# A hybrid decoder layer on one core: block differences on VectorE alone, earlier weight sums and loads, an earlier first w_down split, last rows scaled in two steps

## The chip, the cores and the metric

The kernel runs on one core of a Trainium2 chip. The metric is the device time in microseconds (us). TensorE is PE in the profile's rows (PEld: its weight loads), VectorE is DVE, ScalarE is ACT, GpSimd is POOL, SyncE is SP. A q behind a name (SPq, ACTq) is the engine's sequencer, which issues DMAs.

## The reference, cut to what matters

One layer works on 1024 prompt rows and 32 sample rows together, 1056 rows of 1024 columns in float32. `g_mix` here stands for the three gated branches.

```
x = x + g_mix @ w_o                                   # 1024 x 1024
h = rmsnorm(x, norm_ffn_g) @ w_up                     # 1024 x 5632
hc = dwconv3_causal(h) + conv_f_b ; a, g = split(hc)
x = x + (silu(g) * a) @ w_down                        # 2816 x 1024
y = rmsnorm(x, norm_final_g)
```

## The kernel before, in words

**Precision.** Each float32 operand is split in a high part (ScalarE rounds it: `hi`) and a low part (VectorE subtracts: `lo`), and `three` (L210 to L213) makes a product of three matmuls: high by high, high by low, low by high. For a unit of w_in, w_o or w_down the split is `split_unit`: cast L188 on ScalarE, subtraction L190 on VectorE, which waits in `lows` until `split_lows` issues it.

**W_o.** The 1056 columns are four quarters of 264. 32 steps (`wo_step`, 24 matmuls each) run in the order of the loop at L1536: quarters 0 and 2 first (s = 0, steps 0 to 15), then 1 and 3 (s = 1, steps 16 to 31). The result is added to x in S (L1297 for two quarters of one row block, L1308 for two row blocks of one quarter); ScalarE squares it (L1299, L1302, L1310) and GpSimd or VectorE sums the squares into `acc` (L1303, L1313). `todo` holds what else is issued at a point (step, third of the step): parts of the norm, the first weight loads, sums and splits.

**The norm and z's blocks.** `norm2(c)` makes the second RMSNorm of quarter c: `total` (six tiny matmuls L1217 that sum `acc`, then a short chain L1218 to L241 on VectorE), `spread` (L1229, the scale across partitions), four `scale` items (two L1257 each). w_up is multiplied by a Strassen-like scheme with seven products per pair of halves, so z's four blocks b11, b12, b21, b22 (S, four row blocks by one quarter) are subtracted from each other (`minus`, L1251, four per pair of quarters) and split (`parts`: cast L1246, subtraction L1247). s = 0 stands for quarters 0 and 2, s = 1 for 1 and 3. In norm2(2) all four `minus` are GpSimd's, in norm2(3) two of them.

**W_up.** `entries` holds (j, quarters): the first four are (0, s=0), (1, s=0), (0, s=1), (1, s=1), then j = 2 to 21 with both. Each entry has seven products in the ORDER 1, 2, 6, 5, 7, 3, 4: 12 matmuls each in entries 0 to 3, 24 after that. For each entry `raw_load` fetches four pieces of 256 KB of w_up, `sums` makes the weight sums on GpSimd (L1354 to L1356, and L1371 later), `prepare` splits each weight (L1367 on ScalarE, L1368 on VectorE) three products ahead. `evacuate` reads the result out of PSUM (L1463 on ScalarE for product 1, L1461 on VectorE for the rest); the PSUM tile `pair` has three buffers, so product i + 3 waits for the evacuation of product i. The convolution's taps (L1420, L1424), the gate (L1436, L1437, L1441) follow from a queue `late`.

**W_down.** During the last entry `at_last` loads the first units of w_down and stages the first activations from memory (`loads`) and splits them (`splits`: L1605, L1606). Then 24 units of 24 (or 12) matmuls per 352 columns run, three times. `ahead` splits two units ahead.

**The last rows.** `turn` transposes the result (L1687) and squares it (L1690), `scales` makes the factors, `out` scales by the row's factor and by norm_final_g (`gfin`): L1715 on VectorE, or L1719 on ScalarE followed by L1720 on GpSimd, and stores.

Each engine works in the order of issue; the code is written in the order in which it issues.

Of the kernel before, what the change touches and what calls it, by code (L numbers as in the profile page):

```python
# [9 lines left out]
F32 = mybir.dt.float32  # L10
# [5 lines left out]
P = 128  # L16
D = 1024
# [40 lines left out]
def layer_step(ctx: ExitStack, tc: tile.TileContext, I, O):  # L58
# [297 lines left out]
    with tc.manual_schedule():  # L356
# [848 lines left out]
        def norm2(c):  # L1205
# [56 lines left out]
            if not second:  # L1262
                return total, spread, [
                    scale(0, 0), scale(0, 1), scale(1, 0), scale(1, 1), parts(1, b11), parts(2, b21)
                ]
            dve = nc.vector if s else nc.gpsimd
            return total, spread, [
                scale(0, 0), scale(0, 1),
                minus(b11, b12, b11, dve),
                scale(1, 0), scale(1, 1),  # L1270
                parts(3, b22),
                minus(b12, b22, b12, nc.gpsimd),
                minus(b22, b22, b11, dve),
                parts(6, b22),
                parts(5, b11),
                minus(b21, b21, b22, nc.gpsimd),
                parts(7, b12),
                parts(4, b21),
            ]
# [42 lines left out]
        def raw_load(e):  # L1322
            if e > last or e in raw:
                return
            j = entries[e][0]
            raw[e] = []
            for half in range(2):
                if half and e >= 4:
                    t = v3(S[:, 6 + e % 2, :], KT, P)
                else:  # L1330
                    t = ring.tile([P, KT, P], F32, name="ws", tag="ws", bufs=3)
                t = t[:, 0:4, :], t[:, 4:8, :]
# [28 lines left out]
        def prepare(upto):  # L1361
            while prepared[0] < min(upto, len(steps)):
                e, n = steps[prepared[0]]
                a = raw[e][n]
                t = ring.tile([P, KT, P], F32R, name="wh", tag=("wh", "wl")[prepared[0] % 2], bufs=3)
                hi, lo = t[:, 0:4, :], t[:, 4:8, :]
                nc.scalar.copy(out=hi, in_=a)  # L1367
                nc.vector.tensor_tensor(out=lo, in0=a, in1=f32(hi), op=ALU.subtract)  # L1368
                wform[e, n] = hi, lo
                if n == 1:  # L1370
                    nc.gpsimd.tensor_tensor(out=a, in0=raw[e][2], in1=raw[e][6], op=ALU.subtract)  # L1371
                    if e >= 4:
                        raw_load(e + 1)
                if n == 3 and e < 4:
                    raw_load(e + 1)
                if n == 7 and e >= 4 or n == 4 and e < 4:
                    sums(e + 1)
                if n == 4:
                    raw.pop(e)
                    if e == 0:  # L1380
                        fs.put(wsum.pop(e))
                prepared[0] += 1
# [67 lines left out]
        def evacuate(e, n, ps):  # L1450
            j, ss = entries[e]
            a, m = ss[0], len(ss)
            u = as4(S[:, 2 + e % 2, :]) if e >= 4 else block(S, e % 2 if e < 2 else 0, 2)
            ps = ps[:, a : a + m, :QC]
            s1, u2 = u[:, a : a + m, :], u[:, 2 + a : 2 + a + m, :]

            def cols(half, c):
                at = 2 + (c + a) * QC
                return hb_get(j, half)[:, at : at + m * QC].rearrange("p (s t) -> p s t", t=QC)

            add = lambda out, x: nc.vector.tensor_tensor(out=out, in0=ps, in1=x, op=ALU.add)  # L1461
            if n == 1:
                nc.scalar.copy(out=s1, in_=ps)  # L1463
            elif n == 6:
                add(u2, s1)
            elif n == 2:
                add(cols(0, 0), s1)
            elif n == 5:
                add(s1, u2)
            elif n == 7:  # L1470
                add(cols(1, 2), s1)
                add(u2, u2)
            elif n == 3:
                add(cols(0, 2), s1)
            else:
                add(cols(1, 0), u2)
# [19 lines left out]

        norms = {c: norm2(c) for c in range(4)}

        def plan_norm(at, c, first=0):

            total, spread, items = norms[c]
            slots = {(at, 2): [total], (at + 1, 2): [spread]}
            for i, x in enumerate(items):
                slots[at + 2 + i // 3, i % 3] = [x]
            return slots

        todo = {}
        for at, c in ((12, 0), (16, 2), (28, 1)):
            for key, gos in plan_norm(at, c).items():
                todo.setdefault(key, []).extend(gos)  # L1510
        todo.setdefault((24, 0), []).append(lambda: sums(0))
        todo.setdefault((22, 2), []).append(lambda: raw_load(0))
        for i in range(6):
            todo.setdefault((25 + i // 2, i % 2), []).append(lambda i=i: prepare(i + 1))

        def wo_step(at, w, ps, c):
            wh, wl = w
# [106 lines left out]
        def at_last(n):  # L1624

            if n == 1:
                for c in range(3):
                    for q, g in down_order(c):
                        k0, nk = kg[g]
                        unit_cols(w_down, q * 256, k0=k0, nk=nk, cols=256)  # L1630
            go = {
                1: [load_unit, load_unit, loads[0]],
                5: [lambda: extra_free(6), splits[0], loads[1]],
                7: [lambda: rows_free(0), load_unit, loads[2]],
                3: [splits[1], loads[3], splits[2], loads[4], split_unit],
                4: [lambda: extra_free(7), splits[3], split_lows, loads[5]],
            }
# [5 lines left out]
        ffn_first[1] = [total]  # L1643
# [22 lines left out]


        gfin = fs.get()
        nc.sync.dma_start(out=gfin[:, :D], in_=I["norm_final_g"].partition_broadcast(P))
        extra_free(4)  # L1670
        rows_free(4)

        def finish(c):
# [25 lines left out]
            def scales(a, z):  # L1699
# [3 lines left out]
                    rsqrt(ms, y, tmp, P)  # L1703
                return go

            def out(i, parts=((0, D, True),)):
                def go():
                    t0, n = PIECES[3 * c + i]
# [16 lines left out]
                    fs.put(y)  # L1725
                return go

            return turn, scales, out

        left = list(late)  # L1730
        late.clear()
        for c in range(3):
            turn, scales, out = finish(c)
            work = {}

            def at_slot(q, g, *gos):
# [5 lines left out]
            if c == 0:  # L1742
# [5 lines left out]
                at_slot(0, 4, loads[7])  # L1748
                at_slot(1, 1, splits[7])
                at_slot(1, 2, x_again)  # L1750
            else:
                x_again()
                for i in range(3):
# [14 lines left out]
            for q, g in down_order(c):  # L1768
# [34 lines left out]
        turn, scales, out = before  # L1803
# [42 lines left out]
```

## Time and profile before

| | us |
|---|---|
| median of 3 runs | 1890.14 (1888.81 to 1891.46) |
| the profiled execution | 1889.29 |
| its span in the trace | 1887.5 |
| TensorE busy in the span | 1831.9 |
| W_o, steps 28 to 31, up to W_up's first product | 1098 to 1121 |
| W_up's entries 0 to 3 | 1121 to 1187 |
| W_up's entries 4 to 23 | 1187 to 1602 |
| W_down and the last rows | 1602 to 1887.5 |

The span is counted from the first instruction; the execution's own time is 1.8 us longer. The page shows TensorE nearly full; so the reader looks for stretches in which it is not, and there at who ended its waits. "PEclk" is the clock that was granted to TensorE, 1.00 at full speed.

### The profile page before, as it was taken

The page shows a single profiled execution, that of the slowest core. Times are in us where ns is not written, and L with a number is a line of the kernel's source. Part 1 is how long each engine was busy: PE and PEld are TensorE (multiplying, and loading weights), DVE is VectorE, ACT ScalarE, POOL GpSimd, SP SyncE. Part 2 cuts the span into 40 slices and gives each one's busy share as a digit, 9 for nine tenths or more (in the row PEclk, how much of TensorE's full clock was granted, in tenths as well). Part 3 has the DMA queues.
Part 4 walks back from the last instruction along what each step waited for, and adds up shares of the span by engine and source line. Part 5 has one row for each costly group of instructions (what it writes and reads, how often), then busy time and mean ns, then how long its engine had stood idle before and what let it go on. Part 6 is the DMA issues. An engine that isn't in the chain of part 4 may idle for free. (4 is left out here: it accounts for less than half of the span.)

```text
span 1887.5 us, 31072 instructions
## 1 busy us (share of the span) xinstructions
PE 1831.9 (97%) x12576; PEld 1807.1 (96%) x12576; DVE 1159.2 (61%) x2144; ACT 640.9 (34%) x1045; POOL 384.8 (20%) x475
## 2 busy tenths in 40 slices
PE   8999999999999999999999987999999999899997
PEld 8988999999999999999999986999999999899997
DVE  5577676337633483328436477888988897655433
ACT  6654313221232123211324233334333334444332
POOL 2231100000000000000000344566556654000000
PEclk9999999999999999999999988999999999899999
DMA  8736252125221422133316221323222222776642
GB/s 260 214 106 206 73 175 86 56 68 169 68 59 45 147 93 77 44 120 107 92 35 193 71 79 58 91 71 91 76 74 86 78 79 94 236 230 228 202 156 90
DMA packets 252204, 216.08 MB, mean 114 GB/s; under 512 B 7958, under 2 KB 237150, under 8 KB 252062
## 3 DMA queue, kind: packets, MB, share of 16 engines
q1 hardware_dynamic: 241860, 200.01, 34.3%
q10 hardware_dynamic: 10201, 14.10, 2.2%
q8 instruction: 99, 1.62, 0.3%
q14 instruction: 44, 0.35, 0.1%
HBM read 184.27 MB, written 29.81 MB: 113 GB/s over the span
## 5 line engine op out<-in xcount | busy, mean ns | idle before, releaser
L211 PE MATMUL mm<-zhi,wh 128*128 128x352 f32 x1728 | 560.9, 325 | 0.3 <-ACT zhi L273 0.3
L212 PE MATMUL mm<-zlo,wh 128*128 128x352 f32 x1728 | 558.1, 323 | 1.0 <-POOL zlo L284 1.0
L213 PE MATMUL mm<-zhi,wl 128*128 128x352 f32 x1728 | 557.7, 323 | 0.2 <-DVE wl L190 0.2
L190 DVE TENSOR_TENSOR wl<-ws,wh 128x1024 fp32r<-128x1024 f32 x183 | 223.3, 1222 | 221.9 <-ACT wh L188 221.6
L211 PE MATMUL pair<-zhi,wh 128*128 128x264 f32 (+1 forms) x1096 | 326.0, 297 | 14.1 <-DVE rs L1461 8.8
L212 PEld LDWEIGHTS mm<-zlo,wh 128*128 128x128 f32 x1728 | 324.5, 188 | 2.2 <-POOL zlo L284 1.6
L211 PEld LDWEIGHTS mm<-zhi,wh 128*128 128x128 f32 x1728 | 325.0, 188 | 1.1 <-ACT zhi L273 0.6
L213 PEld LDWEIGHTS mm<-zhi,wl 128*128 128x128 f32 x1728 | 324.6, 188 | 0.5 <-DVE wl L190 0.5
L212 PE MATMUL pair<-zlo,wh 128*128 128x264 f32 (+1 forms) x1096 | 322.9, 295 | 0.0
L188 ACT CAST wh<-ws 128x1024 fp32r<-128x1024 f32 (+1 forms) x184 | 187.3, 1020 | 256.6 <-PE pair L212 97.5
L211 PEld LDWEIGHTS pair<-zhi,wh 128*128 128x128 f32 x1096 | 207.2, 189 | 17.3 <-issue 15.3
L212 PEld LDWEIGHTS pair<-zlo,wh 128*128 128x128 f32 x1096 | 207.5, 189 | 0.0
L213 PE MATMUL pair<-zhi,wh 128*128 128x264 f32 x704 | 201.3, 286 | 0.0
L213 PEld LDWEIGHTS pair<-zhi,wh 128*128 128x128 f32 x704 | 133.9, 190 | 0.0
L211 PE MATMUL pair<-fs,wh 128*128 128x264 f32 (+1 forms) x396 | 119.8, 303 | 3.1 <-ACT wh L188 2.7
L213 PE MATMUL pair<-zhi,wl 128*128 128x352 f32 (+1 forms) x392 | 121.4, 310 | 0.0
L212 PE MATMUL pair<-fs,wh 128*128 128x264 f32 (+1 forms) x396 | 118.5, 299 | 0.0
L844 DVE CUSTOM_DVE_ANT_0 qr<-fs,fs 128x256 f32<-128x256 f32 x256 | 108.4, 424 | 7.3
L211 PE MATMUL pair<-rs,wh 128*128 128x264 f32 (+1 forms) x352 | 104.7, 297 | 4.3 <-DVE rs L1461 3.2
L212 PE MATMUL pair<-rs,wh 128*128 128x264 f32 (+1 forms) x352 | 104.8, 298 | 0.0
L1130 ACT ACTIVATE sig<-mm 128x352 f32<-128x352 f32 x72 | 33.4, 465 | 187.2 <-PE mm L213 186.7
L1143 DVE TENSOR_TENSOR sig<-sig,fs 128x352 f32<-128x352 f32 x48 | 25.2, 525 | 108.0 <-ACT sig L1130 108.0
(333 smaller groups left out, 3276.1 us busy)
## 6 DMA issues: line engine op xcount, KB each, us to landing
ws<-in_w_in SPq DMA_DIRECT2D x88, 512.0 KB
ws<-in_w_down SPq DMA_DIRECT2D x60, 512.0 KB
fs<-q_d SPq DMA_DIRECT2D x32, 512.0 KB
ws<-in_w_up SPq DMA_DIRECT2D x56, 256.0 KB
S<-in_w_up SPq DMA_DIRECT2D x40, 256.0 KB
fs<-in_cache_mem_k SPq DMA_DIRECT2D x16, 512.0 KB
fs<-in_cache_mem_v SPq DMA_DIRECT2D x16, 512.0 KB
act_d<-fs SPq DMA_DIRECT2D x13, 528.0 KB
```

The costliest lines, as they stand in the source:

```text
L188: nc.scalar.copy(out=hi, in_=t)
L190: lows.append(lambda: eng.tensor_tensor(out=lo, in0=t, in1=f32(hi), op=ALU.subtract))
L211: mmul(ps, lhsT=wh, rhs=xh, start=first, stop=False)
L212: mmul(ps, lhsT=wh, rhs=xl, start=False, stop=False)
L213: mmul(ps, lhsT=wl, rhs=xh, start=False, stop=last)
L844: nc.vector.tensor_tensor_reduce(out=att["qr"], in0=q[:, i, :], in1=t[:, 2 * (bb % 2) + mt, :], scale=1.0, scalar=0.0, op0=ALU.mult, op1=A ...
L1130: nc.scalar.activation(out=t, in_=ps, func=AF.Sigmoid)
L1143: nc.vector.tensor_tensor(out=t, in0=t, in1=src[:, r], op=ALU.mult)
```

## The change

- All four `minus` of norm2(2) and norm2(3) are on VectorE.
- `todo` is written point by point: norm2(2)'s items come two per step (from step 18); `raw_load(0)` at step 20, `sums(0)` at step 21, the first six splits at steps 22 to 27, `raw_load(1)` at step 25, `sums(1)` at step 27. norm2(1)'s total moves from behind step 28 into step 29, its spread from behind step 29 into step 30; its two `parts` move behind W_up's products 0 and 1.
- The second halves of the raw weights of entries 1 and 2 lie in S instead of the ring `ws`, so `raw_load(2)` and `raw_load(3)` are issued one entry earlier than before. `sums` of entries 2, 3 and 4 are issued with product 7 (before: product 4 up to entry 3).
- In the last entry of W_up the first unit of w_down is split at product 7 and the second at product 3 (before: the first at product 3, behind two staged pieces, its low part at product 4).
- norm_final_g is loaded in the last quarter of W_down's first third instead of at its start.
- The last three row blocks: VectorE multiplies the first 768 columns by norm_final_g as soon as they are transposed (`scaled`), and the row's factor follows at the end (`out_end`), on ScalarE for the first and third block and on VectorE for the second; the last 256 columns stay in one step on VectorE. All stores are SyncE's.

The last few line numbers shift: L1367 and L1368 are L1371 and L1372 after, L1354 to L1356 are L1358 to L1360, L1371 is L1375, L1461 is L1465, L1605 and L1606 are L1616 and L1617.

```diff
-            dve = nc.vector if s else nc.gpsimd
+            dve = nc.vector
...
-                minus(b12, b22, b12, nc.gpsimd),
+                minus(b12, b22, b12, dve),
                 minus(b22, b22, b11, dve),
...
-                minus(b21, b21, b22, nc.gpsimd),
+                minus(b21, b21, b22, dve),
...
-                if half and e >= 4:
-                    t = v3(S[:, 6 + e % 2, :], KT, P)
+                if half and e in (1, 2):
+                    t = block(S, 1, 4 - 2 * e)
+                    t = t[:, :, 0:P], t[:, :, P : 2 * P]
...
-                    if e >= 4:
+                    if e >= 3:
                         raw_load(e + 1)
-                if n == 3 and e < 4:
-                    raw_load(e + 1)
-                if n == 7 and e >= 4 or n == 4 and e < 4:
+                if n == 3 and e < 2:
+                    raw_load(e + 2)
+                if n == 7 and e:
                     sums(e + 1)
...
-            u = as4(S[:, 2 + e % 2, :]) if e >= 4 else block(S, e % 2 if e < 2 else 0, 2)
+            u = as4(S[:, 2 + e % 2, :]) if e >= 4 else block(S, 0, 2)
...
+        plan_norm(0, (12, 2), (13, 2), [(14, 0), (14, 0), (14, 1), (14, 2), (15, 0), (15, 1)])
+        plan_norm(2, (16, 2), (17, 2), [(18 + i // 2, i % 2) for i in range(13)])
+        rest1 = plan_norm(1, (29, 0), (30, 0), [(30, 1), (30, 2), (31, 0), (31, 1)])
+        at_point(20, 0, lambda: raw_load(0))
+        at_point(21, 2, lambda: sums(0))
...
-                7: [lambda: rows_free(0), load_unit, loads[2]],
-                3: [splits[1], loads[3], splits[2], loads[4], split_unit],
-                4: [lambda: extra_free(7), splits[3], split_lows, loads[5]],
+                7: [lambda: rows_free(0), load_unit, loads[2], split_unit, split_lows],
+                3: [splits[1], loads[3], split_unit, split_lows, splits[2], loads[4]],
+                4: [lambda: extra_free(7), splits[3], loads[5]],
...
+            def scaled(i):
+
+                def go():
+                    n = PIECES[3 * c + i][1]
+                    b = tiles[i][:n].rearrange("p h x -> p (h x)")
+                    nc.vector.tensor_tensor(
+                        out=yo[i][:n, : 6 * P], in0=b[:, : 6 * P], in1=gfin[:n, : 6 * P], op=ALU.mult
+                    )
+                return go
...
+                at_slot(3, 4, gfin_load)
...
                     turn(g - 1, 0, 6)()
+                    scaled(g - 1)()
...
         for i in range(3):
-            out(i, ((0, 512, True), (512, D, i == 2)))()
+            out_end(i)
```

VectorE's order in W_o from step 18 on (S holds x and z, zlo and fs_… the low parts of z's blocks, wh on the left the low part of a weight):

```order
-L1257 SCALAR_TENSOR_TENSOR S<-S,vec,aux 128x264 x8
+L1257 SCALAR_TENSOR_TENSOR S<-S,vec,aux 128x264 x4
+L1251 TENSOR_TENSOR S<-S 128x4x264
+L1257 SCALAR_TENSOR_TENSOR S<-S,vec,aux 128x264 x2
 L1297 TENSOR_TENSOR S<-pair,S 128x2x264
+L1257 SCALAR_TENSOR_TENSOR S<-S,vec,aux 128x264 x2
 L1247 TENSOR_TENSOR zlo<-S,zhi 128x4x264
+L1251 TENSOR_TENSOR S<-S 128x4x264 x2
+L1297 TENSOR_TENSOR S<-pair,S 128x2x264
 L1247 TENSOR_TENSOR fs_10242<-S,fs_10241 128x1056
+L1372 TENSOR_TENSOR wh<-ws,wh 128x512
```

The differences L1251 have entered VectorE's queue between the scalings and the low parts, and the first split weight (L1372) stands ahead of W_o's later additions L1297.

GpSimd's order at the same place (fs_9653 is `acc`, ws the raw weights, fs_10374 and fs_10447 the sums of entry 0):

```order
 L1313 TENSOR_TENSOR fs_9653<-fs_9653,fs_9654 128x264 x4
-L1251 TENSOR_TENSOR S<-S 128x4x264
+L1303 TENSOR_TENSOR fs_9653<-fs_9653,fs_9654 128x2x264 x2
+L1358 TENSOR_TENSOR fs_10374<-ws 128x4x128
+L1359 TENSOR_TENSOR fs_10374<-fs_10374,ws 128x4x128
+L1360 TENSOR_TENSOR ws<-ws 128x512
+L1375 TENSOR_TENSOR ws<-ws,fs_10374 128x512
 L1303 TENSOR_TENSOR fs_9653<-fs_9653,fs_9654 128x2x264
-L1251 TENSOR_TENSOR S<-S 128x4x264 x3
-L1303 TENSOR_TENSOR fs_9653<-fs_9653,fs_9654 128x2x264 x2
-L1354 TENSOR_TENSOR fs_10447<-ws 128x4x128
-L1355 TENSOR_TENSOR fs_10447<-fs_10447,ws 128x4x128
```

Four differences have left GpSimd's queue, and the sums of entry 0 stand ahead of the third of the additions L1303.

VectorE's order at the end of W_up, before (zlo and rs_… on the left of L1606 are low parts of staged activations, wl those of w_down's units, fs_16047 and rs_16151 results of the last entry):

```order
L1461 TENSOR_TENSOR S<-pair,S 128x528
L1461 TENSOR_TENSOR rs_16151<-pair,S 128x528
L1461 TENSOR_TENSOR S<-pair,S 128x528
L1606 TENSOR_TENSOR rs_10795<-S,rs_10794 128x1056
L1606 TENSOR_TENSOR zlo<-S,zhi 128x1056
L1441 TENSOR_TENSOR rs_16016<-rs_16016,S 128x1056
L1461 TENSOR_TENSOR fs_16047<-pair,S 128x528
L1606 TENSOR_TENSOR zlo<-S,zhi 128x1056
L190 TENSOR_TENSOR wl<-ws,wh 128x1024
L1461 TENSOR_TENSOR rs_16151<-pair,S 128x528
L190 TENSOR_TENSOR wl<-ws,wh 128x1024 x2
L1420 SCALAR_TENSOR_TENSOR fs_16197<-fs_16047,vec,fs_16197 128x1024
```

And the same stretch after:

```order
L1465 TENSOR_TENSOR S<-pair,S 128x528
L190 TENSOR_TENSOR wl<-ws,wh 128x1024
L1465 TENSOR_TENSOR rs_16153<-pair,S 128x528
L1465 TENSOR_TENSOR S<-pair,S 128x528
L1617 TENSOR_TENSOR rs_10799<-S,rs_10798 128x1056
L190 TENSOR_TENSOR wl<-ws,wh 128x1024
L1617 TENSOR_TENSOR zlo<-S,zhi 128x1056
L1445 TENSOR_TENSOR rs_16014<-rs_16014,S 128x1056
L1465 TENSOR_TENSOR fs_16045<-pair,S 128x528
L1617 TENSOR_TENSOR zlo<-S,zhi 128x1056
L1465 TENSOR_TENSOR rs_16153<-pair,S 128x528
L190 TENSOR_TENSOR wl<-ws,wh 128x1024
```

The low part of the first unit has moved ahead of product 7's two evacuations, that of the second ahead of the second staged piece; the third still stands behind product 4's evacuation and just ahead of the convolution's taps.

More of the change, by code (lines that the diff above doesn't have):

```diff
@@ L1327, in raw_load @@
             for half in range(2):
-                if half and e >= 4:
-                    t = v3(S[:, 6 + e % 2, :], KT, P)
-                else:
-                    t = ring.tile([P, KT, P], F32, name="ws", tag="ws", bufs=3)
-                t = t[:, 0:4, :], t[:, 4:8, :]
+                if half and e in (1, 2):
+                    t = block(S, 1, 4 - 2 * e)
+                    t = t[:, :, 0:P], t[:, :, P : 2 * P]
+                else:
+                    if half and e >= 4:
+                        t = v3(S[:, 6 + e % 2, :], KT, P)
+                    else:
+                        t = ring.tile([P, KT, P], F32, name="ws", tag="ws", bufs=3)
+                    t = t[:, 0:4, :], t[:, 4:8, :]
                 c0 = half * FF + j * P
@@ L1497, in layer_step, with at_point, plan_norm @@
         norms = {c: norm2(c) for c in range(4)}
-        def plan_norm(at, c, first=0):
+        todo = {}
+        def at_point(step, i, go):
+            todo.setdefault((step, i), []).append(go)
+        def plan_norm(c, t, s, points):
             total, spread, items = norms[c]
[L1502 to L1514, printed above, removed]
+            at_point(*t, total)
+            at_point(*s, spread)
+            for x, point in zip(items, points):
+                at_point(*point, x)
+            return items[len(points) :]
+        plan_norm(0, (12, 2), (13, 2), [(14, 0), (14, 0), (14, 1), (14, 2), (15, 0), (15, 1)])
[3 more added lines that the diff above has]
+        at_point(21, 2, lambda: sums(0))
+        for i, point in enumerate([(22, 0), (23, 0), (24, 1), (25, 0), (26, 0), (27, 0)]):
+            at_point(*point, lambda i=i: prepare(i + 1))
+        at_point(25, 0, lambda: raw_load(1))
+        at_point(27, 1, lambda: sums(1))
         def wo_step(at, w, ps, c):
@@ L1642, in layer_step @@
         total, spread, items = norms[3]
-        ffn_first[1] = [total]
+        ffn_first[0] = rest1[:1]
+        ffn_first[1] = [total, *rest1[1:]]
         ffn_first[3] = [spread]
@@ L1668, in layer_step, with gfin_load @@
         gfin = fs.get()
-        nc.sync.dma_start(out=gfin[:, :D], in_=I["norm_final_g"].partition_broadcast(P))
+        def gfin_load():
+            nc.sync.dma_start(out=gfin[:, :D], in_=I["norm_final_g"].partition_broadcast(P))
         extra_free(4)
@@ L1704, in scales, with out_end @@
                 return go
+            def scaled(i):
[6 more added lines that the diff above has]
+                return go
+            def out_end(i):
+                t0, n = PIECES[3 * c + i]
+                b = tiles.pop(i)[:n].rearrange("p h x -> p (h x)")
+                y, ri = yo.pop(i), st["y3"][:n, i : i + 1]
+                m = min(n, NP - t0)
+                if i % 2:
+                    nc.vector.tensor_scalar(
+                        out=y[:n, : 6 * P], in0=y[:n, : 6 * P], scalar1=ri, scalar2=1.0, op0=ALU.mult, op1=ALU.mult
+                    )
+                else:
+                    nc.scalar.activation(out=y[:n, : 6 * P], in_=y[:n, : 6 * P], func=AF.Copy, scale=ri)
+                nc.vector.scalar_tensor_tensor(
+                    out=y[:n, 6 * P : D], in0=b[:, 6 * P : D], scalar=ri, in1=gfin[:n, 6 * P : D],
+                    op0=ALU.mult, op1=ALU.mult,
+                )
+                for fr in (slice(0, 6 * P), slice(6 * P, D)):
+                    nc.sync.dma_start(out=O["y_prompt"][0, t0 : t0 + m, fr], in_=y[:m, fr])
+                    if m < n:
+                        nc.sync.dma_start(out=O["y_sample"].rearrange("b t d -> (b t) d")[:, fr], in_=y[m:n, fr])
             def out(i, parts=((0, D, True),)):
@@ L1726, in out @@
                 return go
-            return turn, scales, out
+            return turn, scales, out, scaled, out_end
         left = list(late)
@@ L1732, in layer_step @@
         for c in range(3):
-            turn, scales, out = finish(c)
+            turn, scales, out, scaled, out_end = finish(c)
             work = {}
@@ L1802, in layer_step @@
             before = turn, scales, out
-        turn, scales, out = before
         for i in range(3):
```

## The prediction

> **What bounds the kernel now.** I read the page first, then busy time by stage, then TensorE's waits.
>
> ```profile
> span 1887.5 us, 31072 instructions
> PE 1831.9 (97%) x12576; PEld 1807.1 (96%) x12576; DVE 1159.2 (61%) x2144; ACT 640.9 (34%) x1045; POOL 384.8 (20%) x475
> ```
>
> TensorE is busy 1831.9 of 1887.5 us, so only 55.6 us can come from waits. Busy time by stage (columns: PE, PEld, DVE, ACT, POOL busy, granted clock, DMA share, GB/s) shows where they lie.
>
> ```profile
> 1100.00:1122.00 22.00, 15.06 (x105) 14.88 (x104) 13.28 (x24) 5.05 (x9) 6.37 (x6) 0.77 0.28 85
> 1122.00:1187.00 65.00, 47.56 (x343) 46.16 (x342) 50.98 (x82) 25.48 (x41) 32.20 (x31) 0.87 0.24 69
> 1200.00:1600.00 400.00, 400.00 (x3258) 397.94 (x3257) 346.57 (x448) 149.59 (x220) 230.75 (x283) 1.00 0.26 79
> 1600.00:1630.00 30.00, 22.30 (x128) 21.79 (x127) 25.57 (x25) 16.48 (x16) 6.88 (x13) 0.83 0.72 226
> 1630.00:1860.00 230.00, 230.00 (x1450) 229.70 (x1449) 110.28 (x129) 85.25 (x101) 0.10 (x1) 1.00 0.63 202
> ```
>
> From 1200 to 1600 and from 1630 to 1860 TensorE never stops: 0.123 us per matmul of 264 columns (400/3258), 0.159 of 352 (230/1450). The change can win only at W_o's end (6.9 idle in 22), in W_up's entries 0 to 3 (17.4 in 65), where W_down begins (7.7 in 30), and in the last rows. In the first three the clock is below 1 too. TensorE's waits name who was late:
>
> ```profile
> PE pair L211 <- DVE rs L1461: 12.0, 4, 7.4
> PE aux L1217 <- DVE fs L1313: 6.9, 1, 6.9
> PE pair L213 <- DVE wl L190: 5.0, 1, 5.0
> PE pair L211 <- ACT wh L188: 2.7, 1, 2.7
> PE aux L1229 <- DVE y L241: 1.4, 1, 1.4
> ```
>
> Each is VectorE (once ScalarE). So the question is not what TensorE does but when VectorE's queue reaches L1313, L1461 and L190. Two things hold that queue up. First, GpSimd:
>
> ```profile
> 1073.40 2.49 POOL L1251 TENSOR_TENSOR S<-S 128x1056 f32<-128x1056 f32 x1 [15.04 <-DVE S L1257]
> 1077.65 8.57 POOL L1251 TENSOR_TENSOR S<-S 128x1056 f32<-128x1056 f32 x3
> 1096.34 1.74 POOL L1354 TENSOR_TENSOR fs<-ws 128x512 f32<-128x512 f32 x1
> 1098.15 1.63 POOL L1355 TENSOR_TENSOR fs<-fs,ws 128x512 f32<-128x512 f32 x1
> 1146.73 1.26 POOL L1356 TENSOR_TENSOR ws<-ws 128x512 f32<-128x512 f32 x1
> ```
>
> ```profile
> 1084.80 2.54 DVE L1247 TENSOR_TENSOR fs<-S,fs 128x1056 fp32r<-128x1056 f32 x1 [6.00 <-ACT fs L1246]
> 1087.26 1.25 DVE L1247 TENSOR_TENSOR zlo<-S,zhi 128x1056 fp32r<-128x1056 f32 x1
> 1095.45 3.17 DVE L1368 TENSOR_TENSOR wh<-ws,wh 128x512 fp32r<-128x512 f32 x2 [1.28 <-ACT wh L1367]
> 1105.47 0.69 DVE L1308 TENSOR_TENSOR S<-pair,S 128x528 f32<-128x528 f32 x1
> 1107.01 0.90 DVE L1313 TENSOR_TENSOR fs<-fs,fs 128x264 f32<-128x264 f32 x2 [0.84 <-ACT fs L1310]
> ```
>
> L1247 takes 1.25 us with GpSimd idle and 2.54 while the last L1251 runs (to 1086.2); then the two L1368 (0.68 each elsewhere) take 3.17 between L1303, L1354 and L1355, which stretch to 1.74 and 1.63 from about 1.26. I read this as turns: operations with both inputs in SBUF on VectorE and GpSimd run one after the other, and with both queues full they alternate. Second, late weights:
>
> ```profile
> 1144.10 1.31 POOL L1354 TENSOR_TENSOR S<-ws 128x512 f32<-128x512 f32 x1 [12.08 <-DMA ws<-in_w_up]
> 1150.38 2.30 DVE L1251 TENSOR_TENSOR S<-S 128x1056 f32<-128x1056 f32 x1 [6.08 <-POOL S L1251]
> 1153.82 2.89 DVE L1247 TENSOR_TENSOR rs<-S,rs 128x1056 fp32r<-128x1056 f32 x1 [0.19 <-ACT rs L1246]
> 1169.70 1.11 DVE L1368 TENSOR_TENSOR wh<-S,wh 128x512 fp32r<-128x512 f32 x1 [2.88 <-ACT wh L1367]
> ```
>
> GpSimd waits 12.08 us for entry 2's weights; a difference L1251 queued behind its sums comes late, and VectorE, which needs it, stands 6.08 us with W_up's evacuations behind it: that is TensorE's 7.4. The sums of entry 3 repeat this in a smaller way (2.88).
>
> **Part by part. A, W_o's end.** The differences leave GpSimd (2.49 + 8.57 = 11.1 us) for VectorE, where one costs this:
>
> ```profile
> 1135.28 1.25 DVE L1251 TENSOR_TENSOR S<-S 128x1056 f32<-128x1056 f32 x1
> 1136.45 0.68 DVE L1368 TENSOR_TENSOR wh<-S,wh 128x512 fp32r<-128x512 f32 x1
> ```
>
> 1.17 from start to start, 4.7 for four. But sums(0) and its later difference, four GpSimd operations of about 1.27, now come while VectorE has low parts queued, and the first three of sums(1) stand ahead of VectorE's last two L1313. Following VectorE's new order from 1073.2, the fourth scaling's end: four scalings 1.6, four differences 4.7, five low parts 5.9, three L1297 1.9, six weight lows 3.6, two L1308 1.3, two L1313 0.9, together 19.9 us of its own; seven GpSimd turns and parts of turns, 9.2; waits for ScalarE's casts and squares 6.9. `acc` is done at 1109.2 against 1107.9 before. L1217 stands 9 matmuls later in TensorE's queue, so after the wait TensorE has 9 fewer left, at the low clock of this row:
>
> ```profile
> 1109.00:1113.00 4.00, 4.00 (x19) 4.00 (x19) 0.97 (x6) 0.20 (x1) 0.00 (x0) 0.50 0.10 33
> ```
>
> 0.21 us each, 1.9 us. A = +1.3 − 1.9, about **−0.5**. If sums(1) falls behind the L1313 it is −3.5; if one more turn falls ahead, +2. The wait of 6.9 itself stays. The loads' issue is no longer SyncE's hurry: their data was there, and the stores queued behind them gate nothing before step 30.
>
> **B, entries 0 to 3.** Of VectorE's idle 14.0 (65.0 − 50.98), 6.1 and 2.9 + 0.2 go with the late data. The stretch of L1251 and L1247 (2.30 − 1.25, 2.89 − 1.25) goes with GpSimd's two differences: 2.7. The 1.4 at L1229 goes, as sums(1) is over by then. Against that come two differences, 2.3, and one low part of quarter 1 that W_o did before, 1.25. And sums(2) and sums(3), six operations, ran while VectorE stood idle; now they run against a full queue: nothing to 1.17 each, 7.0 in all. Ends: −13.3 + 3.6 = −9.7 without turns, −2.7 with all six; going through the new order I find about four met in full, so B = −9.7 + 4.2 = **−5.5**. What is late next is VectorE itself: the evacuations in entries 1 to 3, short waits at TensorE of 1 to 3 us each.
>
> **C, W_down's begin.** These rows are ScalarE's, VectorE's and SyncE's:
>
> ```profile
> 1604.02 1.04 ACT L188 CAST wh<-ws 128x1024 fp32r<-128x1024 f32 x1
> 1609.45 1.22 DVE L190 TENSOR_TENSOR wl<-ws,wh 128x1024 fp32r<-128x1024 f32 x1
> 1611.73 0.35 SPq L1669 DMA_DIRECT2D rs<-in_norm_final_g  x1
> 1612.17 0.94 SPq L166 DMA_DIRECT2D ws<-in_w_down  x2
> 1618.77 1.05 ACT L188 CAST wh<-ws 128x1024 fp32r<-128x1024 f32 x1 [5.16 <-DMA ws<-in_w_down]
> 1619.85 1.23 DVE L190 TENSOR_TENSOR wl<-ws,wh 128x1024 fp32r<-128x1024 f32 x1 [1.05 <-ACT wh L188]
> ```
>
> The first unit's pieces (1604.0, 1609.5) come some 10 us sooner, so the waits of 2.7 and 5.0 go; the cost, one L190 of 1.2 ahead of product 7's evacuations, is hidden by VectorE's free time before 1602.3. But the fourth unit is next: its load waits for staged pieces ahead of it on SyncE and could start about 2 us sooner, without norm_final_g's 512 KB in front; its low part stands behind the third unit's, three taps of 1.44 and a staged piece, and I get 1617.4 instead of 1619.85. Units one to three no longer hide this. C = **−3.0**; 0 if the load lands no sooner and −10 (2.7 + 5.0 + half-clock) if nothing is late next.
>
> **D, the last rows.**
>
> ```profile
> 1878.93 1.41 DVE L1715 SCALAR_TENSOR_TENSOR fs<-pair,y,rs 128x512 f32<-128x512 f32 x2
> 1879.75 1.01 SPq L1722 DMA_DIRECT2D out_y_prompt<-fs  x2
> 1882.91 0.57 SPq L1724 DMA_DIRECT2D out_y_sample<-rs  x1
> 1883.12 1.26 POOL L1720 TENSOR_TENSOR fs<-fs,rs 128x512 f32<-128x512 f32 x1 [1.27 <-ACT fs L1719]
> 1884.41 0.36 ACTq L1722 DMA_DIRECT2D out_y_prompt<-fs  x1
> ```
>
> The last store is issued at 1884.41 behind GpSimd's second L1720. After, SyncE issues eight stores from about 1879.8; at some 0.5 each the last goes at 1883.6: D = **−0.8** (−1.5 to +0.3). VectorE's three new products lie in its gaps under the last units. W_up's entries 4 to 23 keep their order: nothing.
>
> [...]
>
> **Sum.** −0.5 − 5.5 − 3.0 − 0.8 = −9.8: 1889.29 becomes 1879.5. The median of the runs lies 0.85 above the profiled execution, so 1880.3, rounded to 1880.
>
> **The rivals.** *Turns cost nothing*: GpSimd's sums fall in VectorE's gaps, as sums(2) did before. A loses its 9.2 of turns and with them the wait (6.9 and 9 × 0.21 + its half clock, together about −9.3), B is −9.7, C and D stay: −22.8, 1867 for the median. For it: VectorE is idle 6.9 us there by my own count. Against it: the stretched rows at 1095. *VectorE is the bound anyway*: earlier data only moves the wait; B and C give nothing, −1.3, 1889. For it: 51 of 65 us busy even with the holes. *The clock stays low* (slower): TensorE's many short waits from 1109 to entry 3's end keep the granted clock at 0.50. Then 399 matmuls (63 + 28 × 12) take 0.21 each, 83.8 us and 2 for the norm's small ones, so entry 4 begins at 1195 instead of 1187: +8.1 − 3.8 = +4.3, 1894. It decides by the length of the waits: here half clock followed the waits of 6.9 and 7.4, not that of 1.4 at L1229, and I expect 3.3 at most behind 1109, in between. [...]
>
> **Chances.** Forecast 0.72, free turns 0.13, VectorE bound 0.09, low clock 0.06. Faster 0.85, same 0.09 (a measurement of this kernel tells about 0.2%, 3.8 us, from no change), slower 0.06. The forecast's own terms reach from −4 to −17, 1874 to 1887; down to 1867 the range takes in the free turns: 1867 to 1887.
>
> **What would show it.** In the changed trace: no L1251 on GpSimd; VectorE's at 1.2 to 2.5; a wait of 4 to 8 us at L1217; no wait of GpSimd for w_up over 2 us; several TensorE waits of 1 to 3 us for L1465 up to entry 3; entry 4 near 1181; no wait at W_down's first unit, but one or two behind it, the fourth unit near 1621; the last store issued by SyncE, some 0.8 us nearer to TensorE's last matmul. I am wrong if the wait at L1217 is gone, if W_up's first entries run without waits, or if the clock stays at 0.50 there.

## The result, and the profile after

The changed kernel takes 1877.82 us (median of 4 runs, 1877.39 to 1880.34) against 1889.47 of the kernel before in the same comparison: a ratio of 0.9939, 95% interval 0.9922 to 0.9957, so 11.7 us faster. 1880 was forecast. The profiled execution took 1877.82 us, its span 1875.7.

The head of the changed kernel's page (columns: busy us, share of the span, instructions):

```profile
span 1875.7 us, 31060 instructions
PE 1832.4 (98%) x12576; PEld 1805.9 (96%) x12576; DVE 1169.4 (62%) x2153; ACT 641.7 (34%) x1045; POOL 372.3 (20%) x467
```

TensorE is busy as long as before (1832.4 us against 1831.9); what shrank is its idle time, from 55.6 to 43.3 us. The busy time by stage of the changed kernel, columns as in the prediction:

```profile
1100.00:1122.00 22.00, 15.78 (x113) 15.60 (x112) 12.19 (x24) 4.71 (x9) 7.33 (x7) 0.84 0.48 143
1122.00:1187.00 65.00, 52.69 (x375) 50.77 (x374) 59.95 (x90) 28.56 (x44) 30.08 (x32) 0.89 0.21 60
1600.00:1630.00 30.00, 26.64 (x149) 24.54 (x148) 23.15 (x25) 16.08 (x16) 5.56 (x10) 0.94 0.73 236
```

In W_up's first entries VectorE went from 50.98 to 59.95 busy of 65 us: the idle time behind late data is gone, and VectorE is nearly full. At W_down's begin TensorE is busy 26.6 of 30 us, before 22.3. TensorE's waits in the changed kernel (total, times, longest):

```profile
PE pair L211 <- DVE rs L1465: 6.4, 4, 3.6
PE aux L1217 <- DVE fs L1313: 6.2, 1, 6.2
PE pair L211 <- DVE S L1465: 1.9, 2, 1.2
PE pair L211 <- ACT wh L1371: 1.8, 1, 1.8
PE pair L212 <- DVE rs L1247: 1.4, 1, 1.4
PE pair L213 <- DVE wl L190: 1.4, 2, 0.7
PE pair L211 <- ACT wh L188: 1.3, 2, 1.0
```

The prediction's list of these waits left out a row of before:

```profile
PE pair L211 <- DVE S L1461: 4.3, 2, 3.9
```

With it, the waits for the evacuations fell from 16.3 (12.0 + 4.3) to 8.3 (6.4 + 1.9); those at W_down's begin fell from 5.0 and 2.7 to 1.4 and 1.3, and L1229's is gone. The one at L1217 stayed (6.9, now 6.2). Those for L1371 (ScalarE's cast of a weight) and L1247, both in W_up's first entries, are new.

To size each stage I cut the trace at four instructions that every kernel here has: the first matmul of W_o behind a short wait, the copy of product 1 of entry 0 and of entry 4 out of PSUM (ScalarE), and the first addition of W_down's result (VectorE). Before, in the order of time:

```profile
1012.33 0.39 PE L211 MATMUL pair<-zhi,wh 128*128 128x264 f32 x1 [0.56 <-ACT sig L1130]
1123.29 0.37 ACT L1463 COPY S<-pair 128x264 f32<-128x264 f32 x1
1192.74 0.59 ACT L1463 COPY S<-pair 128x528 f32<-128x528 f32 x1
1653.64 0.88 DVE L1801 TENSOR_TENSOR S<-pair,S 128x704 f32<-128x704 f32 x1
```

And after:

```profile
1012.28 0.39 PE L211 MATMUL pair<-zhi,wh 128*128 128x264 f32 x1 [0.55 <-ACT sig L1130]
1121.10 0.38 ACT L1467 COPY S<-pair 128x264 f32<-128x264 f32 x1
1185.95 0.59 ACT L1467 COPY S<-pair 128x528 f32<-128x528 f32 x1
1642.68 0.88 DVE L1848 TENSOR_TENSOR S<-pair,S 128x704 f32<-128x704 f32 x1
```

The differences give the first two rows of this table, which holds the experiments too (us; the last column is the time up to the span's end):

| kernel | median | W_o | entries 0 to 3 | entry 4 to W_down's first addition | the rest |
|---|---|---|---|---|---|
| before | 1889.47 | 110.96 | 69.45 | 460.90 | 233.9 |
| changed | 1877.82 | 108.82 | 64.85 | 456.73 | 233.1 |
| differences back on GpSimd | 1879.07 | 108.14 | 66.09 | 457.86 | 233.1 |
| loads of entries 2, 3 back | 1876.01 | 106.43 | 66.00 | 456.89 | 233.1 |
| both back | 1882.79 | 106.64 | 71.00 | 457.46 | 233.1 |
| entry 1's sums late | 1876.48 | 106.23 | 64.87 | 456.69 | 233.1 |
| sums as copies | 1870.88 | 106.80 | 59.13 | 457.17 | 233.1 |
| no sums | 1870.14 | 106.66 | 57.55 | 458.01 | 233.2 |
| first split of w_down late | 1882.62 | 109.35 | 64.85 | 460.99 | 233.1 |
| norm_final_g early | 1880.68 | 108.39 | 64.83 | 460.33 | 233.1 |
| last rows as before | 1878.92 | 109.22 | 64.86 | 456.50 | 233.9 |
| L1217 late | 1871.43 | 101.36 | 66.22 | 456.89 | 233.1 |
| L1217 and sums late | 1871.91 | 99.84 | 67.99 | 456.60 | 233.1 |
| these, and entry 4's sums late | 1872.53 | 99.89 | 67.90 | 456.83 | 233.1 |

The four terms measured: W_o −2.1, entries −4.6, W_down's begin −4.2, last rows −0.8. The executions reach the first mark up to 4.1 us apart, whatever the kernel, so the stages are read more finely than the medians. Each row of stages is one execution. Where kernels share a stage's code, W_o differs by up to 1.0 us (108.39 to 109.35), the entries by 0.03, the third stage by 1.4 (456.50 to 457.86) and the last by 0.2.

The second mark is ScalarE's. TensorE's own first matmul of W_up, before and after, is this:

```profile
1120.77 0.29 PE L211 MATMUL pair<-zhi,wh 128*128 128x264 f32 x1
1119.45 0.29 PE L211 MATMUL pair<-zhi,wh 128*128 128x264 f32 x1
```

ScalarE's copy followed it by 2.52 us before, because a cast (L1246) stood ahead of the copy, and follows it by 1.65 now. Cut at TensorE's matmul, W_o gives −1.3 and the entries −5.5.

### The profile page after: what moved, and what is told of

It reads as the page before. It is cut to its first block, busy times and chain, and to the rows that moved or that the text cites. A ratio compares the mean times of both kernels' runs of the same rounds, so it can differ in the third digit from the quotient of the medians.

```text
span 1875.7 us, 31060 instructions
## 1 busy us (share of the span) xinstructions
PE 1832.4 (98%) x12576; PEld 1805.9 (96%) x12576; DVE 1169.4 (62%) x2153; ACT 641.7 (34%) x1045; POOL 372.3 (20%) x467
```

## The experiments

### What won in W_up's first entries: the differences' engine or the early data

First, the six differences back on GpSimd:

```diff
-            dve = nc.vector
+            dve = nc.vector if s else nc.gpsimd
...
-                minus(b12, b22, b12, dve),
+                minus(b12, b22, b12, nc.gpsimd),
...
-                minus(b21, b21, b22, dve),
+                minus(b21, b21, b22, nc.gpsimd),
```

> The changed kernel with the six differences L1251 that it took to VectorE put back on GpSimd; loads, sums and all else as changed. My theory (two-input SBUF operations of VectorE and GpSimd take turns, so it hardly matters which of the two does a difference; what the change won in W_up's first entries is the early data): W_up's start within 1 us of the changed kernel's, entries 0 to 3 up to 3 us longer because two differences queue behind GpSimd's sums, no wait of GpSimd for w_up over 2 us; in all 1878 to 1881. Rival one (the move of the differences is the gain): the 7.4 us wait at L1465 and the late W_up come back, 1884 or more. Rival two (the move cost time, VectorE being full from 1127 to 1185): 1874 or less.

Measured 1879.07 us, ratio to before 0.9942 (0.9927 to 0.9957): the entries grew by 1.2 us, W_o did not grow. So far that fits my theory that the early data won. Next the loads and sums of entries 2 and 3 back at their old points, differences on VectorE:

```diff
-                if half and e in (1, 2):
-                    t = block(S, 1, 4 - 2 * e)
...
-                    if e >= 3:
+                    if e >= 4:
                         raw_load(e + 1)
-                if n == 3 and e < 2:
-                    raw_load(e + 2)
-                if n == 7 and e:
+                if n == 3 and e < 4:
+                    raw_load(e + 1)
+                if n == 7 and e >= 4 or n == 4 and 0 < e < 4:
                     sums(e + 1)
```

> The changed kernel with the raw weights of entries 2 and 3 loaded and summed at the old points (four ring pieces, one entry ahead, sums at product 4); differences on VectorE, entry 1's load and sums at their new points. My theory (the late data was most of the loss in entries 0 to 3, some 9 of VectorE's 14 idle us): GpSimd waits 5 to 12 us for entry 2's weights again, the weight splits of entries 2 and 3 come late and TensorE with them, 1881 to 1885. Rival (only differences queued behind the sums made the late data harmful, and these are gone): within 1.5 us of 1877.8.

Measured 1876.01, 0.9926 (0.9911 to 0.9941), 1.8 less than the changed kernel, though the two intervals overlap. My theory fell: the late data alone costs the entries 1.2 us, and W_o is 2.4 us shorter, for a reason that the next section shows. GpSimd waits as long as it did before, but nothing of VectorE stands behind it. This run's GpSimd and VectorE, in the timeline (the bracket is the idle time before, and who ended it):

```profile
1140.64 2.10 POOL L1355 TENSOR_TENSOR S<-ws 128x512 f32<-128x512 f32 x1 [13.04 <-DMA ws<-in_w_up]
1140.33 1.25 DVE L1251 TENSOR_TENSOR S<-S 128x1056 f32<-128x1056 f32 x1
```

VectorE makes its difference at 1140.33, just as GpSimd begins to sum. Then both edits of above together, and nothing else:

> The changed kernel with both undone: the six differences on GpSimd and the raw weights of entries 2 and 3 loaded and summed at the old points. Entries 0 to 3 (from product 1's evacuation in entry 0 to that in entry 4) took 69.45 us before, 64.85 with the change, 66.09 with the differences back and 66.00 with the loads back. My theory now: the loss needs both, a difference queued on GpSimd behind sums that wait for late weights; so both undone cost far more than 1.2 + 1.2: 68.5 to 70. Rival (two separate small costs that add up, the rest of B's 4.6 lies elsewhere in the change): 67.3. W_up's start as in the run with late loads, about 2.4 us sooner than in the changed kernel, since entry 1's sums still come behind L1313; in all about 1879 to 1881 by the theory, 1877.5 by the rival.

Measured 1882.79, 0.9958 (0.9944 to 0.9973). The entries take 71.0 us, a little more than the 68.5 to 70 that I expected: undoing one costs 1.2, undoing the other 1.2, undoing both 6.2. The timeline of this run shows the chain again:

```profile
1141.54 1.26 POOL L1355 TENSOR_TENSOR S<-ws 128x512 f32<-128x512 f32 x1 [13.36 <-DMA ws<-in_w_up]
1145.32 2.40 POOL L1251 TENSOR_TENSOR S<-S 128x1056 f32<-128x1056 f32 x1
1147.76 2.30 DVE L1251 TENSOR_TENSOR S<-S 128x1056 f32<-128x1056 f32 x1 [7.92 <-POOL S L1251]
```

Weights late, three sums, the difference behind them at 1145.3, VectorE idle for 7.9 us. The loss needs a difference queued behind the sums and sums that wait for data; either part of the change removes most of it (5.0 of 6.2).

### What GpSimd's sums cost beside a full VectorE

Entry 1's sums two steps later:

```diff
-        at_point(27, 1, lambda: sums(1))
+        at_point(29, 2, lambda: sums(1))
```

> The changed kernel with entry 1's weight sums issued at the end of step 29, behind GpSimd's additions of that step, in place of step 27. My theory (turns): the two L1313 that took 2.80 us beside the sums take 0.90, acc is done and L1217 starts 1.9 us sooner (1106.2 in place of 1108.06), the sums run while VectorE waits for TensorE near 1115 to 1120: 1875 to 1876.5. Rival (VectorE is the bound in W_up's entries anyway): L1217 starts sooner but entry 4 does not, 1877.5 to 1878.5. Rival (the sums' time is free): L1217 stays at 1108, no change.

Measured 1876.48, 0.9932 (0.9916 to 0.9949). In the changed kernel VectorE's last additions before L1217 run beside the sums:

```profile
1105.11 2.80 DVE L1313 TENSOR_TENSOR fs<-fs,fs 128x264 f32<-128x264 f32 x2 [0.84 <-ACT fs L1310]
1104.94 1.26 POOL L1358 TENSOR_TENSOR S<-S 128x512 f32<-128x512 f32 x1 [1.84 <-DMA S<-in_w_up]
1106.29 1.33 POOL L1359 TENSOR_TENSOR S<-S,ws 128x512 f32<-128x512 f32 x1
```

and with the sums late they do not:

```profile
1104.64 0.90 DVE L1313 TENSOR_TENSOR fs<-fs,fs 128x264 f32<-128x264 f32 x2 [0.84 <-ACT fs L1310]
1113.35 1.31 POOL L1358 TENSOR_TENSOR S<-S 128x512 f32<-128x512 f32 x1
```

0.90 in place of 2.80, 1.9 us as expected; L1217's wait falls from 6.2 to 4.3, and W_o is 2.6 us shorter. Most of the other 0.7 is the clock: behind L1217, 14 matmuls follow each other at the 0.22 us of half clock, in the changed kernel 20, and at full clock one takes 0.12. The entries stay at 64.87. The run with late loads had its 2.4 us in W_o by the same road: there entry 1's sums began at 1107.4, behind both L1313.

Then the sums of entries 1 to 4 as copies, which leaves the weight sums out:

```diff
+            if 1 <= e <= 4:
+                tt = lambda out, in0, in1, op: nc.gpsimd.tensor_copy(out=out, in_=in0)
...
-                    nc.gpsimd.tensor_tensor(out=a, in0=raw[e][2], in1=raw[e][6], op=ALU.subtract)
+                    if e < 4:
+                        nc.gpsimd.tensor_copy(out=a, in_=raw[e][6])
+                    else:
+                        nc.gpsimd.tensor_tensor(out=a, in0=raw[e][2], in1=raw[e][6], op=ALU.subtract)
```

> The changed kernel with GpSimd's sums of entries 1 to 4 (L1358 to L1360, and L1375 of entries 0 to 3) replaced by copies of one operand: the weight sums of these entries are left out, the products use wrong weights. A copy has one input in SBUF. My theory (operations with two SBUF inputs on VectorE and GpSimd take turns): VectorE's operations beside them keep their own times (L1313 0.45, L1372 0.68, L1247 and L1251 1.25), L1217 starts 1.9 us sooner, entries 0 to 3 take 57 to 62 us in place of 64.85; 1869 to 1874. Rival (any GpSimd access to SBUF stretches VectorE): the stretched rows stay, 1876.5 to 1879. Rival (the turns are there but VectorE's queue has room): L1217 sooner, entries 0 to 3 unchanged, 1875.5 to 1876.5.

Measured 1870.88, 0.9897 (0.9881 to 0.9914), the entries 59.13: the time that the theory gave, but not by its reason. The timeline shows a copy and VectorE's operation behind it:

```profile
1150.18 1.64 POOL L1359 COPY ws<-ws 128x512 f32<-128x512 f32 x1
1151.26 1.09 DVE L1374 TENSOR_TENSOR wh<-ws,wh 128x512 fp32r<-128x512 f32 x1
```

and the groups of the same run the copies that ran alone (count, busy us, mean ns, idle before):

```profile
L1378 POOL COPY ws<-S 128x512 f32<-128x512 f32 x3 | 1.8, 611 | 15.5 <-DVE wh L1374 10.2 <-issue 5.3
```

A copy, with one input in SBUF, is stretched as well: 1.64 us where one alone takes 0.61, and L1374 takes 1.09 in place of 0.68. I read the gain as shorter turns: a copy alone takes 0.61 us, a sum 1.26. So one more kernel left the sums of entries 1 to 4 out altogether:

```diff
+            if 1 <= e <= 4:
+                raw[e] = {1: a11, 2: a12, 6: a22, 5: a12, 7: a21, 3: a11, 4: a22}
+                return
...
+                    if not 1 <= e <= 4:
+                        nc.gpsimd.tensor_tensor(out=a, in0=raw[e][2], in1=raw[e][6], op=ALU.subtract)
```

> The changed kernel with GpSimd's sums of entries 1 to 4 (L1358 to L1360 and L1375) left out altogether; the products use raw weights in their place. In the run with copies a copy took 0.61 us alone but up to 1.6 beside VectorE's full queue, and VectorE's L1372 beside it 1.1 in place of 0.68: copies took turns too, only shorter ones, and half the GpSimd time gave entries 0 to 3 5.7 us (64.84 to 59.13). If the turns cost TensorE in proportion, leaving out the other half gives 4 to 5 more: entries 0 to 3 54 to 55.5, 1865 to 1867.5. Rival (copies cost nothing, what is left is VectorE's own work): 58 to 59.2, 1870 to 1871. Without any GpSimd sum L1372 should take 0.68 and L1247 and L1251 1.25 on average.

Measured 1870.14, 0.99 (0.9883 to 0.9916), the entries 57.55: not in proportion (54 to 55.5), and just short of the rival's 58. VectorE's groups from 1122 to 1187, in the changed kernel (count, busy us, mean ns, idle before):

```profile
L1372 DVE TENSOR_TENSOR wh<-S,wh 128x512 fp32r<-128x512 f32 x12 | 9.9, 829 | 1.9 <-ACT wh L1371 1.9
L1251 DVE TENSOR_TENSOR S<-S 128x1056 f32<-128x1056 f32 x4 | 5.7, 1416 | 0.0
```

and without sums:

```profile
L1375 DVE TENSOR_TENSOR wh<-S,wh 128x512 fp32r<-128x512 f32 x8 | 5.5, 686 | 0.0
L1251 DVE TENSOR_TENSOR S<-S 128x1056 f32<-128x1056 f32 x4 | 5.0, 1249 | 0.0
```

829 falls to 686 and 1416 to 1249 ns, the undisturbed times. One low part is still stretched in these entries, beside the one GpSimd product of the gate that is left there (2.47 us from 1172.29):

```profile
1172.75 2.56 DVE L1375 TENSOR_TENSOR wh<-ws,wh 128x512 fp32r<-128x512 f32 x1 [1.36 <-ACT wh L1374]
```

The sums of entries 1 to 4 together cost the entries 64.85 − 57.55 = 7.3 us. It is not that the sums come late: in the changed kernel ScalarE's casts wait for a sum once, for 0.2 us. VectorE's busy time between the marks falls from 59.8 to 51.5 us. A part of the 7.3 is TensorE's clock: without sums the granted clock is 0.97 in this window, where it was 0.89:

```profile
1122.00:1187.00 65.00, 56.61 (x434) 54.59 (x434) 58.92 (x97) 31.28 (x48) 13.66 (x25) 0.97 0.24 70
```

Of the 57.55 us left TensorE is busy for 49.2.

### What won at W_down's begin

The splits of the first two units at their old places:

```diff
-                7: [lambda: rows_free(0), load_unit, loads[2], split_unit, split_lows],
-                3: [splits[1], loads[3], split_unit, split_lows, splits[2], loads[4]],
-                4: [lambda: extra_free(7), splits[3], loads[5]],
+                7: [lambda: rows_free(0), load_unit, loads[2]],
+                3: [splits[1], loads[3], splits[2], loads[4], split_unit],
+                4: [lambda: extra_free(7), splits[3], split_lows, loads[5]],
```

> The changed kernel with the splits of w_down's first two units at their old places in the last entry; norm_final_g still loaded late. From entry 4 to W_down's first addition the time was 460.90 us before and 456.73 with the change (4.17 won, 3.0 forecast). My theory: nearly all of it is the first unit's split: TensorE waits 2 to 3 us for L188 and about 5 for L190 again at the first unit, 460 to 461 us, 1881 to 1882.5. Rival (part of the gain is SyncE's without the 512 KB of norm_final_g): 458.5 to 459.5, 1879.5 to 1880.5.

Measured 1882.62, 0.9958 (0.9943 to 0.9973), the stage 460.99: the whole 4.2 is gone, and both waits are back:

```profile
PE pair L213 <- DVE wl L190: 4.9, 1, 4.9
PE pair L211 <- ACT wh L188: 2.8, 1, 2.8
```

Then only norm_final_g back at W_down's start:

```diff
+        gfin_load()
         extra_free(4)
...
-                at_slot(3, 4, gfin_load)
```

> The changed kernel with norm_final_g loaded at the start of W_down again. I counted about 2 us for its 512 KB ahead of the fourth unit's load on SyncE. If that load's time decides, the stretch from entry 4 to W_down's first addition grows by 1 to 2 us (457.7 to 458.7), TensorE waiting longer at the fourth or fifth unit: 1878.8 to 1880. Rival (the splits ahead of it on VectorE decide, the load has time to spare): within 0.4 us of 456.73, no change.

Measured 1880.68, 0.9948 (0.9934 to 0.9963), the stage 460.33: 3.6 of the 4.2 is gone, twice what I expected. SyncE's queue and ScalarE in this run's timeline:

```profile
1604.38 0.34 SPq L1683 DMA_DIRECT2D rs<-in_norm_final_g  x1
1604.77 0.98 SPq L166 DMA_DIRECT2D ws<-in_w_down  x2
1612.01 1.04 ACT L188 CAST wh<-ws 128x1024 fp32r<-128x1024 f32 x1 [6.78 <-DMA ws<-in_w_down]
```

and TensorE's wait for that cast:

```profile
PE pair L211 <- ACT wh L188: 5.5, 2, 4.9
```

The same places in the changed kernel:

```profile
1603.15 0.99 SPq L166 DMA_DIRECT2D ws<-in_w_down  x2
1608.46 1.04 ACT L188 CAST wh<-ws 128x1024 fp32r<-128x1024 f32 x1 [2.83 <-PE pair L212]
```

Counted from each run's first mark, the fourth unit's load is issued 2.1 us later (593.0 against 590.9) and its cast starts 4.1 later (600.3 against 596.2), now behind the data and no longer behind TensorE. SyncE's waits in this run (1596 to 1625) name a part of the cause:

```profile
SPq L1683 <- DMA act_d<-rs: 1.6, 1, 1.6
```

I read this as a buffer: norm_final_g's tile takes one from which a store was still reading, and SyncE stands 1.6 us before it can issue that load. This and the issue itself (0.3) make up nearly all of the 2.1; the other 2.0 come behind the issue, where 512 KB more are ahead of the unit's data. With the early load of norm_final_g the wait moves from the first unit to the fourth and keeps most of its cost. Here the gain needs both parts.

### The last rows

```diff
-                    scaled(g - 1)()
...
-            out_end(i)
+            out(i, ((0, 512, True), (512, D, i == 2)))()
```

> The changed kernel with the last three row blocks scaled as before (ScalarE and GpSimd, or VectorE, in one step behind the row's factor). From W_down's first addition to the end it took 233.88 us before and 233.06 with the change, forecast as 0.8. If the two-step scaling is the whole of it, 233.8 to 233.95 comes back and nothing else changes: 1878.4 to 1879. Rival (it is norm_final_g's later load that helps here, too): 233.06 to 233.4.

Measured 1878.92, 0.9945 (0.9931 to 0.996). The stage takes 233.88 us, the time before: the new last rows are the whole 0.8. This run puts back the stores' queue together with the scaling, so the two are not told apart.

### How far TensorE's order alone reaches

L1217 of quarter 1 later:

```diff
-        rest1 = plan_norm(1, (29, 0), (30, 0), [(30, 1), (30, 2), (31, 0), (31, 1)])
+        rest1 = plan_norm(1, (31, 0), (31, 2), [])
...
-        ffn_first[0] = rest1[:1]
-        ffn_first[1] = [total, *rest1[1:]]
+        ffn_first[0] = rest1[:3]
+        ffn_first[1] = [total, *rest1[3:]]
```

> The changed kernel with the matmuls L1217 of quarter 1 six thirds later in TensorE's queue (behind the first third of step 31), its spread at the end of step 31 and its scalings behind W_up's first product. If the wait of 6.2 us is only a matter of TensorE's order, it shrinks to under 1 us, the half clock behind it goes too, and W_up starts some 8 us sooner. What is late next decides: my theory is that VectorE, full from 1127 on, gives back a part, so entry 4 starts 3 to 6 us sooner: 1872 to 1875. Rival (VectorE's work up to entry 4 is the bound, whatever TensorE's order): entry 4 starts within 1.5 us of the changed kernel's, 1876.5 to 1879. Rival (nothing is given back): 1869 to 1870.

Measured 1871.43, 0.9904 (0.9889 to 0.9919): 6.4 us below the changed kernel, and a little below the 1872 to 1875 of my theory; the intervals against the kernel before do not meet. L1217 in this run's timeline:

```profile
1109.45 0.60 PE L1217 MATMUL aux<-ones,fs 128*88 128x1 f32 x6 [0.64 <-DVE fs L1313]
```

and its stages:

```profile
1100.00:1122.00 22.00, 20.75 (x172) 20.14 (x171) 17.91 (x36) 7.68 (x14) 7.53 (x8) 1.00 0.51 153
1122.00:1187.00 65.00, 50.28 (x362) 48.26 (x363) 60.98 (x83) 28.34 (x43) 34.87 (x35) 0.92 0.22 66
```

The wait is 0.64, the granted clock is 1.00 from 1100 to 1122 in place of 0.84, W_o is 7.5 us shorter; the entries give 1.4 back, less than I thought. Now both edits, L1217 at the end of step 30, its spread in step 31, and entry 1's sums late:

```diff
-        rest1 = plan_norm(1, (29, 0), (30, 0), [(30, 1), (30, 2), (31, 0), (31, 1)])
+        rest1 = plan_norm(1, (30, 2), (31, 1), [(31, 2)])
...
-        at_point(27, 1, lambda: sums(1))
+        at_point(29, 2, lambda: sums(1))
...
-        ffn_first[0] = rest1[:1]
-        ffn_first[1] = [total, *rest1[1:]]
+        ffn_first[0] = rest1[:3]
+        ffn_first[1] = [total, *rest1[3:]]
```

> The two edits that helped, together: entry 1's sums behind the additions of step 29, and quarter 1's L1217 at the end of step 30, its spread in step 31, the scalings behind it. Each alone took the time from the wait before W_o to product 1's evacuation from 108.83 to 106.23 and 101.36 us. My theory (VectorE is free again once its queue is ahead of TensorE): no wait at L1217, 100.3 to 101.3 there; entries 0 to 3 between 64.9 and 66.2; 1869.5 to 1871.5. Rival (what comes sooner at W_o's end is given back in the entries, VectorE being full): entries 66.5 to 68, 1871.5 to 1873.

Measured 1871.91, 0.9905 (0.989 to 0.992). W_o is shorter again (99.84), the entries longer (67.99): together 167.8, and 167.6 in the run before. That is what the rival said: what comes sooner at W_o's end is given back in the entries. That VectorE's work is the reason fits its 61.0 busy us of 65 in the run before, but no run takes work from it in this order. The last kernel moved entry 4's sums as well:

```diff
-                if n == 7 and e:
+                if n == 7 and e and e != 3 or n == 4 and e == 3:
```

> The same with entry 4's sums issued at product 4 of entry 3 in place of product 7, so that they do not run beside the taps L1424 and L1428 that delay L1465 (a wait of 4.1 to 4.4 us). Theory: turns are only paid where VectorE's queue is full; it stays full up to entry 4, so the sums take the same turns a few us later and product 6 of entry 4 may wait for its weight: entries 0 to 3 within 1 us of the run without this, 1869 to 1872. Rival (the sums fall into a gap behind the taps): the long wait shrinks by 2 to 3 us, 1867 to 1869.

Measured 1872.53, 0.9909 (0.9892 to 0.9925), the two stages 167.8 once more. There is no gain, as the theory said, and the time lies 0.5 above the 1869 to 1872 that it gave.

## Why the prediction was right, point by point

The sign, the size and the range held: −9.8 was summed, −11.7 measured. By its steps:

**A, forecast −0.5, measured −2.1 by ScalarE's mark, −1.3 by TensorE's first matmul of W_up.** The mechanism was right: the wait at L1217 stayed, and `acc` was not done sooner (L1217 starts 95.7 us behind the first mark before, 95.8 after). Both numbers in it were too high. The turns: VectorE's rows from 1077 to 1108 exceed their undisturbed times by 7.7 us in all, not 9.2, so `acc` is not 1.3 us later. The nine matmuls: from L1217 to W_up's first matmul it takes 12.7 us before and 11.4 after, 1.3 won and not 1.9. The half clock ended at nearly the same time in both (1114.1 and 1113.7), so the matmuls that went from behind L1217 were mostly ones at full clock, of 0.12 us and not 0.21. That entry 1's sums fall ahead of both L1313 was counted and shown: behind them, W_o is 2.6 us shorter.

**B, forecast −5.5, measured −4.6 by ScalarE's mark, −5.5 by TensorE's matmul.** The sum was nearly right (four turns in full would be 4.7, not the 4.2 in it), but a step in it was wrong: "go with the late data". The run with late loads has the 13 us wait of GpSimd back and loses 1.2 us. The loss hung on two conditions at once, and I put it down to one; that the change removed both is why the size came out all the same, which is luck. What the prediction said of the next limit held: VectorE, 60 of 65 us busy, and waits of 1 to 3.6 us for L1465.

**C, forecast −3.0, measured −4.2.** The first unit's waits are gone; the third unit waits 0.3 and 0.7 us, the fourth 1.0 and 0.7, in kind as forecast ("one or two behind it"). But TensorE starts the fourth unit at 1609.6, not near 1621. The late load of norm_final_g was worth more than the 2 us that I gave it: the fourth unit's load starts 2.1 us sooner, and its data come another 2.0 sooner. The bound of "0 if the load lands no sooner" is what the run with the early load came near (0.6 left).

**D, forecast −0.8, measured −0.8**, by the step that was named: SyncE issues the last store 7.2 us behind the end of TensorE's last matmul, before it was ScalarE's at 7.8, and the span ends 0.8 nearer to that matmul.

**The rivals.** Free turns: fell; leaving the sums out wins 7.3 us in the entries. VectorE as the bound: fell for this change, and fits what stops the next one (167.6 to 167.8 us up to entry 4 in three orders). Clock stays low: fell; the half clock came in windows of 7 us or less, which begin within the waits of 6.2 and 3.6 (at 1106.8 and 1171.7) and within a pair of 1.8 and 1.4 (at 1154.7), and 0.89 was granted in the entries, before 0.87. The prediction named the waits of 6.9 and 7.4 as those that half clock followed; before, it also followed the one of 3.9 that its list leaves out (0.53 from 1182.4 to 1186).

**The price of a difference.** VectorE's two differences in a row in the changed kernel:

```profile
1079.04 2.53 DVE L1251 TENSOR_TENSOR S<-S 128x1056 f32<-128x1056 f32 x2
```

2.53 us for two, where one takes 1.25: they stand back to back. L1297 starts behind them at 1081.49, so a difference took 1.22 us of VectorE's queue, and 1.17 was about the right price.

Open: the entries' 57.55 us without sums are not taken apart further. VectorE is busy for 51.5 of them and waits 3.7 for ScalarE's casts (L1374); no run takes work from either.

## What to carry to other kernels

When an engine waits behind another's queue, ask which conditions the loss needs: where it needs two, either cure gives most of the gain and the second adds little (here 5.0 of 6.2 us and 1.2); where a wait only moves to the next consumer, each cure alone is worth little or nothing (here 0.6 and 0 of 4.2). Before moving work from GpSimd to VectorE, look for stretched rows: here the differences cost nearly the same on either side (1.2 us in the entries), and the sums' place in time mattered more (2.6 us for entry 1's). And move what waits in the limiting engine's own order before moving what it waits for: a few lines of TensorE's order were worth 6.4 us here.

## What the runs showed of the hardware that I had not expected

On GpSimd a copy with a single input in SBUF was stretched beside VectorE's two-input operations, too (1.64 us in place of 0.61, and L1374 1.09 in place of 0.68, above), while VectorE's evacuation from PSUM (L1465) kept its 0.42 beside a sum: in the changed kernel one at 1153.74 lies within L1359's 1.60 us from 1153.35.

Half clock came without a long wait. TensorE's waits at W_down's begin in the changed kernel's timeline:

```profile
1609.56 0.43 PE L211 MATMUL pair<-zhi,wh 128*128 128x352 f32 x1 [0.97 <-ACT wh L188]
1611.18 0.43 PE L213 MATMUL pair<-zhi,wl 128*128 128x352 f32 x1 [0.71 <-DVE wl L190]
```

and the stages around them:

```profile
1604.00:1612.00 8.00, 5.59 (x30) 4.69 (x30) 8.00 (x10) 4.60 (x5) 0.00 (x0) 1.00 0.71 215
1612.00:1615.40 3.40, 2.91 (x11) 2.46 (x10) 2.98 (x5) 2.15 (x2) 1.66 (x1) 0.50 1.03 362
```

Waits of 0.97 and 0.71 us within two microseconds, then a clock of 0.50 for 3.4 us. From 1596 to there TensorE has no longer one. What brings the half clock is not shown: in the same trace waits of 1.19, 0.76, 1.09 and 0.70 us from 1140 to 1150 left the clock at 1.00. The prediction named half clock behind the waits of 6.9 and 7.4 us, and none behind that of 1.4.
